# Block products for the input projections of a transformer layer, with q, k, v and pooled features kept in DRAM

## The chip, the core and the metric

The kernel runs on one core of a Trainium2 chip. The metric is the device time of one execution in microseconds (us), the median of several runs. The engines are TensorE (PE, with its weight loads as PEld), VectorE (DVE), ScalarE (ACT), GpSimd (POOL) and SyncE (SP, which issues most loads). Each engine works through its own list of instructions in a fixed order.

## What is computed

One layer over 1024 tokens of width 1024. A combined input projection feeds three token mixers; each has its output projection and a gate; the sum goes through w_out; a SwiGLU FFN follows.

```python
n = rmsnorm(h, norm_mix_pre)
proj = n @ w_in                     # 512 pool, 3 x 512 q k v, 256 xq, 3 x 1024 gates
gates = sigmoid(proj[..., o2:]).reshape(b, s, 3, d)
y_pool = pool_mixer(p_in, w_pool_mix, pool_scale) @ w_pool_o    # windows 2, 4, 8, 16
y_sb = stick_breaking_attention(q, k, v) @ w_sb_o               # 8 heads of 64, causal
y_x = memory_cross_attention(xq, rmsnorm(mem, norm_mem), w_mem_kv) @ w_x_o   # 4 heads, 256 tokens
merged = gates[:, :, 0] * y_pool + gates[:, :, 1] * y_sb + gates[:, :, 2] * y_x
h = h + rmsnorm(merged @ w_out, norm_mix_post)
gu = rmsnorm(h, norm_ffn_pre) @ w_ffn_in
h = h + rmsnorm((silu(gu[..., :D_FF]) * gu[..., D_FF:]) @ w_ffn_out, norm_ffn_post)
```

In the stick-breaking attention a weight is sigmoid(z_ts) times the product of (1 - sigmoid(z_tj)) over the keys between s and t; there is no softmax.

## The kernel before

Tokens are reversed in time and stand in two chunks c of 512 columns; features lie on partitions, in eight tiles k of 128. Precision comes from splitting: each operand is a high part (rounded to the matmul's format, ScalarE) and a low part (the rest, VectorE or POOL), and `mm3` issues three matmuls, lines 164 to 166:

```python
nc.tensor.matmul(ps, lh, rh, start=first, stop=False, skip_group_check=onto)
nc.tensor.matmul(ps, lh, rl, start=False, stop=False, skip_group_check=onto)
nc.tensor.matmul(ps, ll, rh, start=False, stop=last, skip_group_check=onto)
```

`split` (lines 145 to 160) loads a weight tile of 128 x 512 and makes its two halves, `wh` on ScalarE (L158) and `wl` (L159) on VectorE or, where the call says so, on POOL. `project` (from line 301) makes one tile of 128 output features for both chunks: 2 chunks x 8 k x 3 = 48 matmuls of 512 columns.

The stages, in the order of the program:

1. x is loaded, scaled and split while the pooling part of w_in is multiplied with it; the sum of squares gives the row scale (`rms_rows`, with `diag` at L190).
2. x is loaded again and normalised (`normalise`, L241 and L245) into the tiles nh and nl, beside the memory's K and V (mk, mv: matmuls of 256 columns).
3. xq (2 tiles by `project`), then the pool mixing (L399 to L428: window sums on VectorE, one small product, result in SBUF), then the memory attention: `scores` with a softmax made of two sigmoids and a reciprocal (L455 to L459), `recalled`.
4. The first branch's gates (8 tiles by `project`), each with its product with w_pool_o (12 matmuls a chunk).
5. V: 2 chunks x 8 k x 4 row blocks x 3 = 192 matmuls of 512 columns, result in SBUF.
6. The head loop, four head pairs p. Each projects q and k (`project`, `stack_q`, `stack_k`), then goes through eight units (t2, e). `sticks` makes the scores (L558, L559), two sigmoids, the scan on VectorE (L573) and the multiplication (L583); `values` transposes (L596), splits (L169, L170) and multiplies with V (L608, L611); L350 adds the halves. `sticks` runs one unit ahead of `values`. Gate tiles of the branches 1 and 2 stand between: one after the projections and the rest after the units. Finished gates go to DRAM.
7. The merge (from L642): the head outputs (oh, ol) with w_sb_o, the memory attention's (xo, from DRAM) with w_x_o, times the gates loaded from DRAM; then w_out.
8. The FFN, already in blocks of seven products (`product`, `opening`, and the loop after it).

What stands in which order on an engine is set by the tile scheduler, which follows the program's order, takes blocks under `tc.high_priority()` earlier, and keeps the loads that go through `load` in program order on SP's queue. Buffers come from pools (act 32, a 16, b1 8, b2 8, c 12, d 6, r 4 tiles; eight PSUM banks as pa 3, pz 2, pt 2, pv 1).

## Time and profile before

| | |
|---|---|
| runs | 1520.4 us median of 3 (1519.17 to 1521.04) |
| profiled execution, its own time | 1520.77 us |
| its span, first to last instruction | 1519.1 us |
| PE busy | 1470.4 us, 97% |
| VectorE busy | 1013.5 us, 67% |
| ScalarE busy | 693.8 us, 46% |
| POOL busy | 476.2 us, 31% |
| mean granted TensorE clock | 0.990 |
| moved by DMA | 203.23 MB, 134 GB/s |

Shares are of the span, the time between the first and the last instruction. The engines work side by side, so the shares don't add up; PEld is shown apart from PE since the weight load of one matmul can run beside the matmul ahead of it. A wait in the profile names the instruction that waits and, behind the arrow, the one that released it.

### The profile page before, as it was taken

The numbers are of one execution on the slowest core, as the hardware profiler recorded it, in microseconds if no ns is written. First come the engines' busy times: TensorE is split into PE (matmuls) and PEld (weight loads), VectorE is DVE, ScalarE is ACT, GpSimd is POOL, SyncE is SP. The second block draws the span as 40 slices with busy tenths as digits, with TensorE's granted clock in tenths as the row PEclk, the third lists the DMA queues.
The fourth block names the chain that finished last, engine by engine and source line by source line (L and its number), as shares of the span: only waits on it lengthen the run. The fifth ranks groups of instructions, "written<-read, shape, count | busy, mean of one in ns | idle before, by whom it ended". The sixth has DMA issues, their size and how long they took to land.

```text
span 1519.1 us, 20437 instructions
## 1 busy us (share of the span) xinstructions
PE 1470.4 (97%) x6878; PEld 1217.4 (80%) x6878; DVE 1013.5 (67%) x1552; ACT 693.8 (46%) x1375; POOL 476.2 (31%) x747
## 2 busy tenths in 40 slices
PE   9799999999999999998999989999999999999996
PEld 7678888888888888886788778888888887788875
DVE  8996996327687475766624478675566666578475
ACT  7454665235565454552234664223333333444452
POOL 7554342044454444445565530000011112000011
PEclk9999999999999999999999999999999999999998
DMA  6432222332231322217665453443465555664344
GB/s 223 133 99 67 70 90 79 107 100 71 56 84 49 90 60 69 68 55 230 199 201 178 156 189 118 157 142 125 132 194 194 193 187 201 231 192 146 105 152 160
DMA packets 101034, 203.23 MB, mean 134 GB/s; under 512 B 12720, under 2 KB 14272, under 8 KB 100928
## 3 DMA queue, kind: packets, MB, share of 16 engines
q1 hardware_dynamic: 81216, 147.36, 32.0%
q0 software_dynamic: 19136, 53.51, 10.2%
q8 instruction: 54, 0.88, 0.2%
q10 hardware_dynamic: 576, 1.05, 0.2%
...
HBM read 148.39 MB, written 48.76 MB: 130 GB/s over the span
## 4 chain that ended last, share of the span: by engine, by line
PE 82%; DVE 8%; DMA 4%; issue 3%; ACT 2%; POOL 1%; SPq 0%; DVEq 0%; POOLq 0%; ACTq 0%
PE pa L164 16%; PE pa L165 16%; PE pa L166 16%; PE pz L166 5%; PE pz L164 5%; PE pz L165 5%; PE pt L166 3%; PE pt L164 3%; PE pt L165 3%; PE pt L596 2%; PE pv L611 1%; PE pz L559 1%; PE pz L558 1%; PE pv L608 1%; DMA d<-gt 1%
## 5 line engine op out<-in xcount | busy, mean ns | idle before, releaser
L166 PE MATMUL pa<-act,wl 128*128 128x512 f32 (+1 forms) x716 | 280.7, 392 | 1.7 <-DVE wl L159 1.7
L165 PE MATMUL pa<-act,wh 128*128 128x512 f32 (+1 forms) x716 | 281.3, 393 | 0.0
L164 PE MATMUL pa<-act,wh 128*128 128x512 f32 (+1 forms) x716 | 280.4, 393 | 0.6 <-ACT act L708 0.6
L159 POOL TENSOR_TENSOR wl<-ws,wh 128x512 fp32r<-128x512 f32 x132 | 181.1, 1374 | 238.1 <-ACT wh L158 224.8
L158 ACT CAST wh<-ws 128x512 fp32r<-128x512 f32 (+1 forms) x199 | 122.9, 618 | 194.3 <-PE pa L165 59.5
L166 PEld LDWEIGHTS pa<-act,wl 128*128 128x128 f32 x716 | 135.4, 189 | 27.9 <-DVE wl L159 2.3
L164 PEld LDWEIGHTS pa<-act,wh 128*128 128x128 f32 x716 | 135.4, 189 | 26.9 <-ACT act L708 0.9
L165 PEld LDWEIGHTS pa<-act,wh 128*128 128x128 f32 x716 | 135.5, 189 | 25.4
L849 POOL DMA_DIRECT2D ff<-c x44 | 23.8, 540 | 222.9 <-DVE c L904 130.1
L159 DVE TENSOR_TENSOR wl<-ws,wh 128x512 fp32r<-128x512 f32 (+1 forms) x67 | 52.7, 789 | 59.5 <-ACT wh L158 38.6
L708 ACT CAST wh<-b 128x512 fp32r<-128x512 f32 x82 | 50.9, 620 | 88.2 <-PE pa L165 51.6
L169 ACT CAST d<-pt 128x512 fp32r<-128x512 f32 (+1 forms) x96 | 53.1, 559 | 70.9 <-PE pt L596 47.1
L170 DVE TENSOR_TENSOR d<-pt,d 128x512 fp32r<-128x512 f32 (+1 forms) x96 | 60.7, 637 | 34.6 <-ACT d L169 34.1
L708 ACT CAST d<-b 128x512 fp32r<-128x512 f32 x66 | 40.8, 621 | 93.8 <-PE pt L165 46.2
L709 DVE TENSOR_TENSOR d<-b,d 128x512 fp32r<-128x512 f32 x66 | 45.4, 691 | 54.5 <-ACT d L708 54.5
L573 DVE TENSOR_TENSOR_SCAN r<-d,zero 128x513 f32<-128x513 f32 (+1 forms) x64 | 60.1, 945 | 28.1 <-POOL d L566 27.6
L175 POOL TENSOR_TENSOR rc<-rv,mhalf 128x1 f32<-128x1 f32 (+2 forms) x15 | 14.5, 967 | 202.1 <-DVE rv L1011 199.4
L164 PE MATMUL pa<-a,wh 128*128 128x512 f32 x192 | 75.6, 395 | 0.8 <-DVE c L892 0.8
L166 PE MATMUL pa<-a,wl 128*128 128x512 f32 x192 | 75.0, 392 | 0.5 <-DVE wl L159 0.5
L708 ACT CAST wh<-ws 128x512 fp32r<-128x512 f32 x44 | 27.4, 622 | 90.3 <-DVE ws L883 45.7
L583 DVE TENSOR_TENSOR b<-b,r 128x512 f32<-128x512 f32 (+1 forms) x96 | 63.4, 669 | 7.4 <-ACT d L169 0.5
L709 DVE TENSOR_TENSOR wl<-b,wh 128x512 fp32r<-128x512 f32 x82 | 56.2, 685 | 15.1 <-ACT wh L708 10.5
...
## 6 DMA issues: line engine op xcount, KB each, us to landing
b<-in_w_ffn_in_dram SPq DMA_DIRECT2D x88, 256.0 KB, 2.7
ws<-in_w_gate_dram SPq DMA_DIRECT2D x48, 256.0 KB, 2.6
gt<-g POOLq DMA_DIRECT2D x48, 256.0 KB, 2.8
d<-gt SPq DMA_DIRECT2D x48, 256.0 KB, 3.4
ws<-in_w_ffn_in_dram SPq DMA_DIRECT2D x44, 256.0 KB, 2.7
ff<-c POOLq DMA_DIRECT2D x44, 256.0 KB, 3.1
b<-ffS SPq DMA_DIRECT2D x44, 256.0 KB, 2.6
b<-ff SPq DMA_DIRECT2D x33, 256.0 KB, 3.2
```

The lines of the kernel that those rows point to most:

```text
L158: nc.scalar.copy(wh[:, :n], ws[:, :n])
L159: lo.tensor_sub(wl[:, :n], ws[:, :n], wh[:, :n].bitcast(F32))
L164: nc.tensor.matmul(ps, lh, rh, start=first, stop=False, skip_group_check=onto)
L165: nc.tensor.matmul(ps, lh, rl, start=False, stop=False, skip_group_check=onto)
L166: nc.tensor.matmul(ps, ll, rh, start=False, stop=last, skip_group_check=onto)
L169: nc.scalar.copy(hi, ps)
L170: nc.vector.tensor_sub(lo, ps, hi.bitcast(F32))
L573: nc.vector.tensor_tensor_scan(ex[:, lo : C + 1], rest[:, lo : C + 1], zero.broadcast_to([P, C + 1 - lo]), 1.0 if c == i // 4 else carry[i ...
L583: nc.vector.tensor_mul(sg[:, lo:], sg[:, lo:], carry[i][:, lo:C])
L596: nc.tensor.transpose(ptr[:, col + n * P : col + (n + 1) * P], att[i, j // 4][:, (j % 4) * P : (j % 4 + 1) * P], ident,)
L708: nc.scalar.copy(hi, src)
L709: eng.tensor_sub(lo, src, hi.bitcast(F32))
```

## The change

The blocks. The normalised x is no longer one set of tiles but a 2 x 2 matrix of blocks (first index: chunk; second: half of the features), and four sums of blocks are made beside it: S1 = 21 + 22, S2 = S1 - 11, S4 = 12 - S2, S3 = 22 - S2. Two neighbouring weight tiles over both chunks are then made of seven products (`pairs`), each with 4 k x 3 = 12 matmuls of 512 columns; sums of weight blocks are made on VectorE, halves of the weights on VectorE or POOL. xq, q, k and the first branch's gates go this way, 1 + 2 + 2 + 4 pairs. V does too (`v_product`), with V's weights as the moving operand in halves of 256 columns.

DRAM. Raw pooled features, xq, q, k, v and the mixed pool features (with their low parts) are written to DRAM by POOL's queue and come back through SP's: `fetch(p, c)` brings a head pair's q and k in loads of 64 rows, `pooled` and `recall` their own.

Order. Three gate half tiles (`early`) run before the sums are made. Memory attention and pool mixing become steps (`aside`) that run between products. The gates of branches 1 and 2 become 58 steps of 12 matmuls, 4 ahead of the heads, 46 inside them in proportion to the transposes of a unit, 8 behind. The product with w_pool_o stands in the merge. Softmax takes one Exp per block with its sum, then a multiplication by the reciprocal of that sum. In `sticks` the ones and the carry are set by POOL in the scan's result and no longer in its input.

```diff
@@ the blocks of x; normalise() goes
+    A = {n: [None] * HK for n in ("11", "12", "21", "22", "S1", "S2", "S3", "S4")}
+    def normed_x(k, c, t):
+        load(t, x[k, c])
+        nc.vector.scalar_tensor_tensor(t, t, gain(G_PRE, k), rbc[c], ALU.mult, ALU.mult)
+        return t
...
+    early(0)
+    sums, a22 = [None] * HK, [None] * HK
+    for q in range(HK):
+        room = t_d if q < 3 else t_r
+        sums[q], a22[q] = normed_x(q, 1, room()[:, :C]), normed_x(q + HK, 1, room()[:, :C])
+        nc.vector.tensor_add(sums[q], sums[q], a22[q])
+        A["S1"][q] = parts(sums[q], t_act(), t_act(), nc.vector if q % 2 else nc.gpsimd)
+    xq_raws = [quarters(w_xq, 0)]
+    early(1)
+    xq_raws.append(quarters(w_q, 0))
+    early(2)
+    for q in range(HK):
+        nc.vector.tensor_sub(sums[q], sums[q], a11[q])
+        A["S2"][q] = parts(sums[q], t_a(F32R), t_a(F32R))
...
@@ two weight tiles by seven products
+    def opening(raw, sink):
+        (b11, b12), (b21, b22) = raw
+        X, Y = ps_a(), ps_a()
+        product(X, w_parts(b11, nc.gpsimd), "11", True)
+        p1 = copied(X)
+        product(Y, w_parts(b21, nc.gpsimd), "12", True)
+        nc.vector.tensor_add(p1, Y, p1)
+        sink(0, 0, p1)
+        return X
+
+    def pairs(jobs, raws=None, pool=("S4", "S3", "22")):
...
+            X, Y = opened[j], ps_a()
+            t = b11
+            nc.vector.tensor_sub(t, b12, t)
+            product(Y, some(t, "S1"), "S1", True)
+            s5 = copied(Y)
+            aside()
+            nc.vector.tensor_sub(t, b22, t)
+            product(X, some(t, "S2"), "S2")
+            s2 = copied(X)
+            product(Y, some(b22, "S4"), "S4")
+            nc.vector.tensor_add(s2, Y, s2)
+            sink(0, 1, s2)
+            aside()
+            nc.vector.tensor_sub(b12, b22, b12)
+            product(X, some(b12, "S3"), "S3")
+            nc.vector.tensor_add(s5, X, s5)
+            sink(1, 1, s5)
+            nc.vector.tensor_sub(b21, b21, t)
+            if len(opened) == j + 1 < len(jobs):
+                opened.append(opening(raws[j + 1], jobs[j + 1][1]))
+            product(X, some(b21, "22"), "22")
+            sink(1, 0, X)
+            aside()
...
@@ q, k, xq to DRAM and back
+    def to_parts(dst, m):
+        def sink(c, i, t):
+            hi, lo = parts(t, t_d(F32R)[:, :C], t_d(F32R)[:, :C])
+            for u, d in zip((hi, lo), dst[m + i][c]):
+                nc.gpsimd.dma_start(d, u)
+        return sink
+    def stacked(dst, src, e):
+        r = slice(e * HD, (e + 1) * HD)
+        load(dst[:HD], src[e][r])
+        load(dst[HD:], src[1 - e][r])
...
@@ softmax
-            nc.scalar.activation(ew[:, :MEM], z[:, :MEM], AF.Sigmoid, bias=st[:, 0:1], scale=SCALE)
-            nc.vector.reciprocal(ew[:, MEM:], ew[:, MEM:])
...
+            nc.scalar.activation(
+                ew[:, zs], z[:, zs], AF.Exp, bias=st[:, 2 + i : 3 + i], scale=SCALE,
+                accum_out=st[:, 4 + i : 5 + i],
+            )
...
@@ V
+                mm3(
+                    ps, ah[:, bs], al[:, bs], wh[:, qs], wl[:, qs],
+                    first and k == 0 and b % 2 == 0, k == HK - 1, not first or b % 2 == 1,
+                )
...
@@ heads
-        accs = project(w_q, p, lo=nc.gpsimd)
...
-        gates(todo[first[p] : first[p] + 1])
...
+    def stick_unit(p, t2, e):
+        if (t2, e) == (0, 0):
+            fetch(p, 1)
+        if (t2, e) == (2, 0) and p < 3:
+            fetch(p + 1, 0)
+        return sticks(*heads[p], t2, e)
...
+        done += share[t2]
+        upto = inside * done // total
+        fill(upto - filled)
+        filled = upto
...
@@ merge
+            pp_ = ps_t()
+            for q in range(4):
+                qs = slice(q * P, (q + 1) * P)
+                mm3(pp_, pwh[:, qs], pwl[:, qs], ph[q][c], pl[q][c], q == 0, q == 3)
...
+            nc.vector.tensor_mul(gt[0], pp_, gt[0])
```

Three places where the order of an engine's list is another. First VectorE ahead of the memory's V, before; `wl_847` is the low half of the first weights of V of the memory, L241 and L245 are the normalisation and its low parts, L409 the window sums of the pool mixing:

```order
L241 SCALAR_TENSOR_TENSOR d_830<-d_830,g_sb_99,r_458 128x512
L159 TENSOR_TENSOR wl_787<-ws_784,wh_786 128x512
L241 SCALAR_TENSOR_TENSOR d_837<-d_837,g_sb_99,r_458 128x512
L245 TENSOR_TENSOR act_820<-d_816,act_819 128x512
L409 TENSOR_TENSOR c_1106<-c_648 128x527
L409 TENSOR_TENSOR c_1126<-c_647 128x527
L409 TENSOR_TENSOR c_1143<-c_650 128x527
L159 TENSOR_TENSOR wl_847<-ws_844,wh_846 128x512
L241 SCALAR_TENSOR_TENSOR d_880<-d_880,g_sb_99,r_521 128x512
L245 TENSOR_TENSOR act_834<-d_830,act_833 128x512
```

and in the changed kernel, where L256 and L251 are the normalisation and its low parts, L195 the scale's diagonal and L164 the low halves of weights:

```order
L256 SCALAR_TENSOR_TENSOR d_633<-d_633,g_sb_99,r_458 128x512
L256 SCALAR_TENSOR_TENSOR d_640<-d_640,g_sb_99,r_458 128x512
L251 TENSOR_TENSOR act_504<-c_500,act_503 128x512
L191 TENSOR_SCALAR rv_732<-pt_457 128x2
L164 TENSOR_TENSOR wl_785<-ws_782,wh_784 128x512
L251 TENSOR_TENSOR act_518<-c_514,act_517 128x512
L251 TENSOR_TENSOR act_630<-d_626,act_629 128x512
L251 TENSOR_TENSOR act_644<-d_640,act_643 128x512
L195 TENSOR_SCALAR r_736<-ident_101,rc_734 128x128 x2
L164 TENSOR_TENSOR wl_803<-ws_800,wh_802 128x512
L164 TENSOR_TENSOR wl_835<-ws_832,wh_834 128x512
L164 TENSOR_TENSOR wl_853<-ws_850,wh_852 128x512
```

The window sums and the second chunk's normalisations no longer stand between the low halves.

Second PE in the last head pair, before; L596 are transposes, L608 and L611 the products with V, L164 to L166 the merge's products, which the scheduler drew in between:

```order
L608 MATMUL pv_7061<-d_7067,a_3225 128x256
L611 MATMUL pv_7061<-d_7066,a_3225 128x256
L608 MATMUL pv_7061<-d_7067,a_3219 128x128
L611 MATMUL pv_7061<-d_7066,a_3219 128x128
L608 MATMUL pv_7061<-d_7080,a_3237 128x256
L611 MATMUL pv_7061<-d_7079,a_3237 128x256
L608 MATMUL pv_7061<-d_7080,a_3231 128x256
L611 MATMUL pv_7061<-d_7079,a_3231 128x256
L165 MATMUL pa_7524<-b2_7441,wh_7480 128x512
L166 MATMUL pa_7524<-c_7440,wl_7481 128x512
```

and in the changed kernel, where L887 are transposes and L899 and L902 the products with V:

```order
L887 MATMUL pt_7383<-ident_101,b2_7243 128x128
L887 MATMUL pt_7383<-ident_101,b2_7254 128x128
L887 MATMUL pt_7383<-ident_101,b2_7243 128x128
L899 MATMUL pv_7289<-d_7295,a_5788 128x256
L902 MATMUL pv_7289<-d_7294,a_5788 128x256
L899 MATMUL pv_7289<-d_7295,a_5790 128x128
L902 MATMUL pv_7289<-d_7294,a_5790 128x128
L899 MATMUL pv_7289<-d_7308,a_5784 128x256
L902 MATMUL pv_7289<-d_7307,a_5784 128x256
L899 MATMUL pv_7289<-d_7308,a_5786 128x256
L902 MATMUL pv_7289<-d_7307,a_5786 128x256
```

Here transposes and products with V follow one another without any other work between.

Third PE at the passage to the merge, before; `pz` is the memory attention's product with w_x_o, `b1` its operand from DRAM:

```order
L166 MATMUL pz_7503<-b1_7456,wl_7475 128x512
L164 MATMUL pz_7503<-b1_7460,wh_7474 128x512
L608 MATMUL pv_7120<-d_7126,a_3237 128x256
L611 MATMUL pv_7120<-d_7125,a_3237 128x256
L608 MATMUL pv_7120<-d_7126,a_3231 128x128
L611 MATMUL pv_7120<-d_7125,a_3231 128x128
L165 MATMUL pz_7503<-b1_7461,wh_7474 128x512
L166 MATMUL pz_7503<-b1_7460,wl_7475 128x512
```

and in the changed kernel, where `pt` is the product with w_pool_o, `a` its operand from DRAM, and `pa` the head outputs' product with w_sb_o:

```order
L899 MATMUL pv_7472<-d_7478,a_5784 128x256
L902 MATMUL pv_7472<-d_7477,a_5784 128x256
L899 MATMUL pv_7472<-d_7478,a_5786 128x128
L902 MATMUL pv_7472<-d_7477,a_5786 128x128
L169 MATMUL pt_7728<-a_7618,wh_7648 128x512
L170 MATMUL pt_7728<-a_7620,wh_7648 128x512
L169 MATMUL pt_7776<-a_7652,wh_7648 128x512
L170 MATMUL pt_7776<-a_7654,wh_7648 128x512
L171 MATMUL pa_7741<-c_7668,wl_7643 128x512
L169 MATMUL pa_7741<-c_7672,wh_7642 128x512
```

The memory attention's product comes later, and the pool product stands among the first of the merge.

## Rows read from the trace of the kernel before

**Rows 1.** Page, part 1: busy time, share of the span and instructions of each engine.

```profile
PE 1470.4 (97%) x6878; PEld 1217.4 (80%) x6878; DVE 1013.5 (67%) x1552; ACT 693.8 (46%) x1375; POOL 476.2 (31%) x747
```

**Rows 2.** By stage: length; busy (count) PE, PEld, DVE, ACT, POOL; clock, DMA share, GB/s.

```profile
48.00:120.00 72.00, 62.55 (x296) 52.46 (x296) 71.50 (x104) 34.21 (x64) 40.88 (x32) 0.93 0.40 114
...
120.00:340.00 220.00, 219.99 (x1060) 183.91 (x1059) 139.80 (x261) 104.42 (x223) 66.49 (x130) 1.00 0.29 86
...
340.00:680.00 340.00, 339.41 (x1811) 290.07 (x1810) 230.46 (x316) 182.99 (x396) 153.03 (x312) 1.00 0.24 65
...
680.00:760.00 80.00, 71.83 (x314) 57.13 (x313) 51.49 (x78) 21.30 (x40) 42.07 (x39) 0.98 0.68 214
...
925.00:1280.00 355.00, 355.00 (x1568) 293.98 (x1567) 232.42 (x366) 122.48 (x211) 43.17 (x80) 1.00 0.52 169
```

**Rows 3.** PE's timeline: first and last of a run of 256-column matmuls.

```profile
68.09 0.28 PE L164 MATMUL pa<-act,wh 128*128 128x256 f32 x1
...
70.12 0.28 PE L166 MATMUL pa<-act,wl 128*128 128x256 f32 x1
```

**Rows 4.** Groups by form: weight loads, busy time, mean ns, idle before.

```profile
L165 PEld LDWEIGHTS pa<-act,wh 128*128 128x128 f32 x716 | 135.5, 189 | 25.4
```

**Rows 5.** PE's waits: line, releaser; us in total, times, longest.

```profile
PE pa L165 <- DVE wl L159: 5.1, 2, 4.1
...
PE pt L194 <- DVE r L190: 4.1, 2, 2.4
...
PE pa L164 <- DVE d L683: 3.4, 2, 2.9
...
PE pz L165 <- DMA b<-xo: 2.9, 2, 2.0
...
PE pa L164 <- ACT c L647: 1.3, 1, 1.3
```

**Rows 6.** VectorE's timeline, from the normalisations' start to the awaited weight half.

```profile
46.97 2.73 DVE L241 SCALAR_TENSOR_TENSOR d<-d,g_sb,r 128x512 f32<-128x512 f32 x4
...
73.84 0.68 DVE L159 TENSOR_TENSOR wl<-ws,wh 128x512 fp32r<-128x512 f32 x1
```

**Rows 7.** Groups of the page and by form: busy, mean ns, idle before.

```profile
L459 DVE RECIPROCAL c<-c 128x256 f32<-128x256 f32 x32 | 54.4, 1727 | 2.6 <-ACT c L455 2.2
...
L709 DVE TENSOR_TENSOR wl<-b,wh 128x512 fp32r<-128x512 f32 x82 | 56.2, 685 | 15.1 <-ACT wh L708 10.5 <-issue 4.0
...
L159 POOL TENSOR_TENSOR wl<-ws,wh 128x512 fp32r<-128x512 f32 x132 | 181.1, 1374 | 238.1 <-ACT wh L158 224.8
...
L573 DVE TENSOR_TENSOR_SCAN r<-d,zero 128x513 f32<-128x513 f32 (+1 forms) x64 | 60.1, 945 | 28.1 <-POOL d L566 27.6
...
L583 DVE TENSOR_TENSOR b<-b,r 128x512 f32<-128x512 f32 (+1 forms) x96 | 63.4, 669 | 7.4 <-ACT d L169 0.5
...
L170 DVE TENSOR_TENSOR d<-pt,d 128x512 fp32r<-128x512 f32 (+1 forms) x96 | 60.7, 637 | 34.6 <-ACT d L169 34.1
...
L573 DVE TENSOR_TENSOR_SCAN r<-d,r,zero 128x513 f32<-128x513 f32 x32 | 41.5, 1302 | 7.8 <-ACT d L562 7.8
...
L350 DVE TENSOR_TENSOR b<-pv,t 64x256 f32<-64x256 f32 x32 | 13.4, 420 | 31.5 <-ACT t L349 31.1
...
L849 POOL DMA_DIRECT2D ff<-c x44 | 23.8, 540 | 222.9 <-DVE c L904 130.1 <-DVE c L890 92.7
```

**Rows 8.** Chain that ended last: eight transposes of the head loop in a row.

```profile
374.76 0.87 PE pt L596 x8
```

**Rows 9.** Engines in a stretch of the memory attention, columns as in rows 2.

```profile
160.00:200.00 40.00, 40.00 (x211) 34.03 (x210) 38.93 (x71) 25.42 (x58) 14.07 (x32) 1.00 0.20 64
```

**Rows 10.** Timelines of VectorE and of POOL at 626 us, head loop.

```profile
626.50 1.40 DVE L583 TENSOR_TENSOR b<-b,r 128x384 f32<-128x384 f32 x1
...
625.78 1.69 POOL L159 TENSOR_TENSOR wl<-ws,wh 128x512 fp32r<-128x512 f32 x1 [0.20 <-ACT wh L158]
```

**Rows 11.** DMA issues of the page: x, KB each, median us to landing.

```profile
d<-gt SPq DMA_DIRECT2D x48, 256.0 KB, 3.4
```

More of the change, by code (lines that the diff above doesn't have):

```diff
@@ new lines, in hybrid_block, with fetch @@
+    to_values(0, 1, s2)
+    aside()
+    sub2(b12, b22, b12)
+    v_product(X, two(b12), "S3")
+    for i in range(2):
+        nc.vector.tensor_add(s5[i], X[i], s5[i])
+    to_values(1, 1, s5)
+    aside()
+    sub2(b21, b21, b11)
+    v_product(X, two(b21), "22")
+    to_values(1, 0, X)
+    while background:
+        aside()
+    heads = {}
+    def fetch(p, c):
+        if c == 0:
+            heads[p] = [[[None] * NC for _ in range(2)] for _ in range(3)]
+        qst, kh, kl = heads[p]
+        for e in range(2):
+            for tiles in (qst, kh, kl):
+                tiles[e][c] = t_c(F32R)[:, :C]
+            stacked(qst[e][c], q_d[p][c], e)
+            twice(kl[e][c], k_d[p][c][1], e)
+            twice(kh[e][c], k_d[p][c][0], e)
+        if p % 2 == 0 and c == 1:
+            for j in range(KT - 1, -1, -1):
+                v = v_sb[j][p // 2] = t_a(F32R)
+                load(v, v_d[j][p // 2])
@@ new lines, in hybrid_block @@
+    mix_h, mix_l = split(w_mix)
+    background += [pooled(g, c) for g in range(4) for c in (1, 0)] + [lambda: fetch(0, 0)]
+    pairs([(lambda m=m: quarters(w_gate, m), to_gate(0, m)) for m in range(0, KT, 2)], pool=())
+    for q in range(HK):
+        u = normed_x(q, 1, t_d()[:, :C])
+        A["21"][q] = parts(u, t_act(), t_act())
+    later = [
+        (b * KT + m, half, c)
+        for b in (1, 2)
+        for m in range(KT)
+        for half in range(2)
+        for c in range(1 if b == 1 and m < EARLY else 0, NC)
+    ]
@@ new lines, in hybrid_block, with gate_load, fill @@
+    gate_units = list(dict.fromkeys((t, half) for t, half, _ in later))
+    gate_w = {}
+    def gate_load():
+        if gate_units:
+            t, half = gate_units.pop(0)
+            ws = wpool.tile([P, C], F32, tag="ws", name="ws", bufs=3)
+            load(ws, w_gate[t, half])
+            gate_w[t, half] = ws
+    def fill(n):
+        for _ in range(n):
+            t, half, c = later.pop(0)
+            if gate_w[t, half].__class__ is not tuple:
+                gate_w[t, half] = w_parts(gate_w[t, half], nc.gpsimd)
+                gate_load()
+            gate_step(t, half, c, gate_w[t, half])
@@ new lines, in hybrid_block @@
+    fill(FILL_FIRST)
+    inside = len(later) - FILL_LAST
+    done = filled = 0
+    share = [15, 11, 7, 3]
+    total = 2 * 4 * sum(share)
+    o_sb = [[None] * NC for _ in range(4)]
+    units = [(p, t2, e) for p in range(4) for t2 in range(4) for e in range(2)]
+    def stick_unit(p, t2, e):
[4 more added lines that the diff above has]
+        return sticks(*heads[p], t2, e)
+    ahead = stick_unit(*units[0])
@@ L641, in hybrid_block @@
+    merge_w = []
+    fill(len(later))
+    for c in range(NC):
+        for g in range(4):
+            for dst, d in zip((ph, pl), ph_d[g][c]):
+                dst[g][c] = t_a(F32R)
+                load(dst[g][c], d)
+        if c == 0:
+            w_merge(0)
     oh = [[None] * NC for _ in range(4)]
```

483 lines of the change are left out of this document (281 added, 202 removed).

## The prediction

> **What bounds the kernel now.** The profile was read from the coarse to the fine: the page's busy times, the time by stage, PE's list of waits, then timelines of single stretches. TensorE is busy for 97% of the span, VectorE for 67% [rows 1]. The table by stage says where the missing 3% lies [rows 2]. From 120 to 340 us (projections, memory attention, first gates) PE has no gap, and none from 925 to 1280 (FFN); in the head loop (340 to 680) it lacks 0.6 of 340 us. The gaps before the FFN are at 48 to 120 us (9.45 us idle, clock 0.93) and at 680 to 760 (8.2 us idle, clock 0.98). So a matmul saved in a gapless stretch shortens the run by its spacing, and work saved on another engine by nothing. In the FFN 1568 matmuls of 512 columns take 355.0 us: 0.2264 us each [rows 2]. Those of 256 columns, at the full clock, follow one another in 0.1194 us (17 intervals from 68.09 to 70.12) [rows 3], half of it.
>
> **The matmuls.** In blocks, two weight tiles over both chunks take 7 products of 12 matmuls, not 96. Pairs: xq 1, q 2, k 2, first gates 4; 9 x 12 = 108 matmuls of 512 columns fewer. V loses its 192 and gets 7 products x 4 row blocks x 4 k x 3 = 336 of 256 columns. The product with w_pool_o (16 x 12) moves from the gates to the merge, its count as before. Sum: -300 x 0.2264 = -67.9, +336 x 0.1194 = +40.1, so **-27.8 us**. V alone gives 3.4 of them, since its 1/8 fewer columns come in twice as many matmuls, each with a weight load. That spacing hides the load: one is recorded at 189 ns, over 119 [rows 4].
>
> The Trainium skill (TensorE: Matmul & The Clock Gate, "The mechanism" in Part 3) says that a weight load overlaps matmuls in flight only when the row groups differ. By that, each of V's would cost 0.189 + 0.119, 336 of them 103.5 us, and the sum would be 63 us higher, slower than before; [rows 3, 4] speak against it, since those loads fill all rows and are hidden.
>
> **Start (48 to 120 us).** PE's longest waits are here: 5.1 us for a low weight half from VectorE, 4.1 us for the scale's diagonal [rows 5]. Between 46.97 and 73.84, the awaited half, VectorE runs normalisations and the pool mixing's multiplications and sums [rows 6]. The order shows the pool mixing gone from here and only eight normalisations left, about 10 us of work in place of 27. At stake are 9.45 us idle and about 5 us of half clock (7% of 72): 14.5. What comes late next are the sums S1 to S4, which all four pieces of VectorE, ScalarE and POOL work must make before the pairs; three gate tiles (72 matmuls, 16 us) lie ahead of them as cover. I take **-10**, nearer to the whole than to nothing, as the row that waited longest goes; bounds 0 and -14.5.
>
> **Softmax and pool mixing.** Of VectorE's work 32 reciprocals at 1.73 us go, 54 us [rows 7]; two more activation-table loads come. Both lie where PE has no gap: 0. The pairs add VectorE and POOL work: per pair (84 matmuls, 19.0 us of PE) 13 VectorE operations at 0.69 = 9.0 us, on POOL 5 subtractions at 1.37 and 8 stores at 0.54 = 11.2 [rows 7]. Covered, with the background steps between; without cover, VectorE would add some 9 us a pair. Stores and reloads through DRAM bring some 40 MB (80 tiles of 256 KB out, as much back in) to a stretch that moved 41 (220 us at 86 GB/s, 340 at 65), a DMA share of about 0.5; the FFN has no gap at 0.52 [rows 2]: 0.
>
> **Head loop.** Here the cover shrinks. PE's own part: 288 transposes at 0.109 [rows 8], 256 matmuls of 256 columns, 96 of 512, the rest by width, 103 us. Gate pieces: 58 x 12 x 0.2264 = 158. In all 261 us, where before the q and k projections and more gates made it 340. VectorE's part stays: scans 60.1 + 41.5, multiplications 63.4, lows 60.7 less 16 x 0.68 for memory attention, additions 13.4: 228 us [rows 7], 87% of 261 where it was 68% of 340. Walking through PE's order with these durations, VectorE's due work runs ahead of PE's in three stretches without gate pieces: the middle of the second head pair (37.3 us of PE to 46.6 of VectorE), the end of the third (25.1 to 35.9) and of the fourth (5.6 to 18.4): 9, 11 and 13 us. Scores are made one unit ahead, which absorbs part; before, such rises were 3 to 5 us and cost 0.6 in 340. I take **+15**, about half; bounds 0 and +33. A fetch lands in about 3.4 us [rows 11], and one unit of attention or a gate piece (2.7 us) lies ahead of each: four bare ones would cost 14, within the bounds.
>
> **Merge (680 to 760 us).** PE waits 2.9 us for the memory attention's tiles from DRAM, 3.4 for a VectorE product or half, 1.3 for ScalarE [rows 5]. Sixteen pool products (16 x 12 x 0.2264 = 43 us, moved, not added) now come with it: the order puts the first of them among the last values, and a block of the merge asks for 2.15 MB in 13.6 us instead of 1.9 MB in 8.2. At stake are 8.2 us idle and 1.6 of clock. I take **-5**, since the one of 2.9 us for VectorE, ahead of w_out, is not touched; bounds 0 and -8. New joints between stages (pairs to V, V to pairs, first fetch): **+3**, from waits of 0.6 to 1.3 us for single operands [rows 5]; bounds 0 and +8.
>
> **Sum.** -27.8 - 10 + 15 - 5 + 3 = -24.8. The profiled execution took 1520.8 us (span 1519.1), 0.4 over the median of 1520.4, so the same sum serves both: **1496 us**, 1.6% faster. About 0.2% (3 us) is what a measurement of this kernel tells from no change.
>
> **Rivals.**
> 1. *The gaps come back elsewhere* (0.2). The S sums are late by as much as the weights were, the merge waits for 2.15 MB a block: only the matmuls and half of start and merge are won. -27.8 - 4 + 18 + 3 = -11, **1510**. For it: the start's VectorE is busy for 71.5 of 72 us [rows 2], and S1 is the first thing that the pairs use. Against it: 16 us of gate matmuls ahead.
> 2. *The head loop keeps PE full* (0.2). -27.8 - 12 + 0 - 5 + 3 = -42, **1479**. For it: at 160 to 200 us VectorE was busy for 38.93 of 40 us and PE for all 40 [rows 9]. Against it: there PE's work did not depend on that of VectorE unit by unit.
> 3. *VectorE becomes the bound of the head loop* (0.06), the slower side. A multiplication of 384 columns took 1.40 us where a POOL subtraction lay beside it (POOL's ran from 625.78 to 627.47) [rows 10]; the mean of all 96 is 0.67 [rows 7]. If every one took 1.40, that is 96 x 0.73 = 70 more: VectorE 298 us, at a share of 0.97 a stretch of 307, so +46: -27.8 - 10 + 46 - 5 + 3 = +6, **1527**. It goes over to slower where the loop loses 40, that is from 292 us of VectorE, 0.67 us more for each multiplication. Against it: POOL has two wide subtractions for a gate tile, as before, and the mean says that few multiplications met one.
> 4. *The removed matmuls are not on the path* (0.04): projections wait for VectorE or POOL for as long as they got shorter, **1519**. Against it: 9.0 and 11.2 of 19 us.
>
> The Trainium skill (SBUF — State Buffer, "Who interferes with whom") says that a VectorE instruction with two SBUF inputs and a GpSimd instruction that reads SBUF exclude one another for the whole instruction. That is rival 3's mechanism, and the 1.40 us agree; which of the two waits it leaves to the order of issue. By its rule, with every one of the 96 hit and losing, the time would be 1527; the mean of 0.67 us bears out a small part of that.
>
> **How the numbers follow.** My forecast has 0.5, rival 1 and 2 each 0.2, rival 3 0.06, rival 4 0.04. The bounds: start and merge at their best and no loss in the heads give 1470, the heads' +33 alone 1514, with half of start lost 1519. The range of 8 in 10 reaches to both neighbours, **1474 to 1515**. Faster by over 0.2%: the forecast, rivals 1 and 2, less a little for a stack of losses in one of them, 0.89; within: 0.04; slower: 0.07.
>
> **What would show it.** Matmuls of 512 columns down by 300, of 256 up by 336, V's at 0.12 us. Between 48 and 120 us under 5 us idle, none of it for a weight half. In the pairs PE without gaps. In the head loop VectorE at 80 to 85%, and PE waiting 10 to 20 us in all for the multiplication before a transpose or for the lows before a value, most of it where no gate pieces lie. In the merge no wait for the memory attention's tiles. Wrong, if V's matmuls come at over 0.2 us, if PE waits in the pairs for S sums over 10 us, or if multiplications in the head loop have a mean over 1.2 us.

## The result and the profile after

| | before | changed |
|---|---|---|
| median | 1519.8 us | 1535.2 us |
| profiled execution (span) | 1520.8 (1519.1) | 1532.7 (1531.0) |
| granted clock, mean | 0.990 | 0.984 |

The ratio is 1.0097, with a 95% interval of 1.0074 to 1.012: 1% slower, where 1.6% faster had been forecast. One run of the changed kernel was disturbed (5106 us) and is left out; the other three lie between 1532.7 and 1536.9 us.

To see where the time went, the trace of both kernels was cut at the first 256-column matmul, the last one of the memory's V, the first score and the last value product. In each part every matmul was counted at its undisturbed spacing (0.227 us for 512 columns, 0.175 for 384, 0.1195 for 256, 0.109 for 128): that is the work. What its start and the next one's start lie further apart is the loss (waits, half clock, late starts). The 1.1 us ahead of the first matmul and the 14.8 us from the start of the last one on are the same in both kernels and stand in no part.

| part | before: work + loss | changed: work + loss | change of the loss |
|---|---|---|---|
| up to the memory's K | 49.3 + 9.6 | 49.3 + 10.2 | +0.6 |
| K and V of the memory | 12.0 + 12.4 | 11.6 + 0.3 | -12.1 |
| from there to the first score | 256.2 + 4.3 | 247.3 + 43.9 | +39.6 |
| heads | 341.9 + 5.2 | 271.1 + 28.4 | +23.2 |
| merge to the end | 779.1 + 33.2 | 831.3 + 21.7 | -11.5 |
| sum | 1438.5 + 64.7 | 1410.6 + 104.5 | +39.8 |

The work fell by 27.9 us, the loss rose by 39.8: +11.9, which is the difference of the spans. Matmuls of 512 columns fell from 5776 to 5476 and those of 256 rose from 514 to 850, as forecast. The rest of this text is about the 39.8.

The busy times of the page of the changed kernel, against [rows 1]:

```profile
PE 1453.5 (95%) x6914; PEld 1201.0 (78%) x6914; DVE 1042.6 (68%) x1593; ACT 705.2 (46%) x1405; POOL 530.2 (35%) x754
```

The same view by stage as [rows 2] (length; busy and count of PE, PEld, DVE, ACT, POOL; clock, DMA share, GB/s), first over the old stretch from 48 to 120 us, then over the parts as they lie now:

```profile
48.00:120.00 72.00, 53.13 (x256) 43.30 (x255) 68.76 (x74) 33.03 (x63) 47.82 (x42) 0.86 0.43 139
...
73.00:123.00 50.00, 31.16 (x109) 23.52 (x108) 49.97 (x50) 19.77 (x37) 32.09 (x22) 0.76 0.29 98
...
123.00:364.00 241.00, 228.45 (x1237) 195.69 (x1236) 175.40 (x328) 125.73 (x268) 112.15 (x141) 0.99 0.54 164
...
364.00:663.00 299.00, 282.12 (x1536) 236.55 (x1535) 224.48 (x321) 173.93 (x384) 144.50 (x291) 0.99 0.40 128
...
663.00:770.00 107.00, 107.00 (x463) 87.30 (x463) 55.46 (x77) 22.05 (x37) 50.65 (x43) 0.99 0.63 198
```

Between 73 and 123 us PE issues only 109 matmuls, at a clock of 0.76, and VectorE is never free: 49.97 of 50 us for 50 operations, a mean of 1.0 us where [rows 7] show 0.69 for a subtraction of that size. The merge (663 to 770) has no gap any more; before, it had two of the longest waits of [rows 5].

PE's waits (line, releaser; us in total, times, longest), against [rows 5]:

```profile
PE pa L169 <- ACT g L512: 10.3, 1, 10.3
...
PE pa L169 <- ACT wh L250: 6.1, 5, 2.3
...
PE pa L169 <- DVE d L532: 5.0, 1, 5.0
...
PE pv L899 <- DVE b L371: 4.6, 5, 1.6
...
PE pt L887 <- DVE d L175: 3.3, 4, 1.5
...
PE pv L899 <- DVE d L175: 3.1, 5, 1.4
...
PE pa L169 <- DVE d L357: 2.4, 1, 2.4
...
PE pz L589 <- DMA r<-xq: 2.2, 1, 2.2
```

The 5.1 us for the low weight half and most of the 4.1 for the diagonal are gone, as is the wait for `xo`. In their place stand 10.3 us for a gate's sigmoid (L512), 5.0 put down to a block of a sum (L532), and in the heads the addition that frees the bank of the values (L371) and the low parts (L175).

The name L532 misleads. The matmul that waits, at 83.26 us, belongs to the second gate tile, which needs no sum; what it needs is the high half of its weights, and the cast of that (L163) ended at the same moment. ScalarE's timeline:

```profile
82.06 0.62 ACT L250 CAST act<-d 128x512 fp32r<-128x512 f32 x1 [4.64 <-DVE d L525]
...
82.59 0.61 ACT L163 CAST wh<-ws 128x512 fp32r<-128x512 f32 x1
```

The cast stands behind one that waited for VectorE's sum S1 (L525) until 82.06, and its own weights had landed only at 81.05, behind the eight x tiles and four xq weights on SP's queue.

V's matmuls in the new form, PE's timeline, first and last of 33 in a row:

```profile
234.23 0.28 PE L169 MATMUL pa<-wh,act 128*128 128x256 f32 x1
...
238.07 0.28 PE L171 MATMUL pa<-wh,act 128*128 128x256 f32 x1
```

32 intervals in 3.84 us: 0.120 us each, as in [rows 3].

What happened at 85 us, first VectorE's timeline, where L536 is the subtraction for S4 and L251 a low part:

```profile
83.76 1.76 DVE L251 TENSOR_TENSOR act<-r,act 128x512 fp32r<-128x512 f32 x1
...
85.44 1.75 DVE L536 TENSOR_TENSOR c<-act,d 128x512 f32<-128x512 f32 x1
...
87.12 5.60 DVE L536 TENSOR_TENSOR c<-act,d 128x512 f32<-128x512 f32 x1
...
92.64 0.68 DVE L532 TENSOR_TENSOR d<-d,c 128x512 f32<-128x512 f32 x1
```

and POOL's over the same stretch (L164 and L251 are low parts, L513 a store):

```profile
84.93 1.72 POOL L164 TENSOR_TENSOR wl<-ws,wh 128x512 fp32r<-128x512 f32 x1
...
86.59 0.56 POOL L513 DMA_DIRECT2D gt<-g  x1
...
87.18 1.29 POOL L164 TENSOR_TENSOR wl<-ws,wh 128x512 fp32r<-128x512 f32 x1
...
88.41 3.76 POOL L251 TENSOR_TENSOR act<-d,act 128x512 fp32r<-128x512 f32 x3
```

POOL is never free from 84.93 to 92.2 us, and from 87.18 on it does four subtractions in a row. A subtraction of VectorE that takes 0.69 us alone took 5.60 from 87.12 on: it ended 0.55 us after the last of POOL's. From 94.6 to 107 us the two engines took turns instead, seven operations each, every one 1.7 to 1.8 us long; one of either:

```profile
97.93 1.75 POOL L164 TENSOR_TENSOR wl<-ws,wh 128x512 fp32r<-128x512 f32 x1
...
98.44 1.78 DVE L251 TENSOR_TENSOR a<-d,a 128x512 fp32r<-128x512 f32 x1
```

Over the part from 58 to 123 us VectorE's operations took 65.4 us; at the shortest tenth of the times that operations of the same form take in this trace they would take 40.1.

### The profile page after: what moved, and what is told of

It is laid out like the page before. It is cut to its first block, busy times and chain, and to the rows that moved or that the text cites. A ratio compares the mean times of both kernels' runs of the same rounds, so it can differ in the third digit from the quotient of the medians.

```text
span 1531.0 us, 21083 instructions
## 1 busy us (share of the span) xinstructions
PE 1453.5 (95%) x6914; PEld 1201.0 (78%) x6914; DVE 1042.6 (68%) x1593; ACT 705.2 (46%) x1405; POOL 530.2 (35%) x754
## 4 chain that ended last, share of the span: by engine, by line
PE 74%; DVE 10%; issue 5%; DMA 4%; POOL 3%; ACT 3%; SPq 1%; POOLq 0%; DVEq 0%; ACTq 0%
PE pa L169 14%; PE pa L171 14%; PE pa L170 14%; PE pz L171 5%; PE pz L169 5%; PE pz L170 5%; PE pt L169 3%; PE pt L171 3%; PE pt L170 3%; DVE r L868 2%; DMA ws<-in_w_gate_dram 1%; PE pt L887 1%; POOL wl L251 1%; PE pv L169 1%; PE pv L170 1%
## 5 line engine op out<-in xcount | busy, mean ns | idle before, releaser
L169 PE MATMUL pa<-act,wh 128*128 128x512 f32 (+1 forms) x572 | 227.1, 397 | 24.7 <-ACT g L512 10.3
L170 PE MATMUL pa<-act,wh 128*128 128x512 f32 (+1 forms) x572 | 225.2, 394 | 0.0
L171 PE MATMUL pa<-act,wl 128*128 128x512 f32 (+1 forms) x572 | 223.0, 394 | 2.2 <-POOL wl L164 2.2
L250 ACT CAST wh<-b 128x512 fp32r<-128x512 f32 x159 | 98.2, 621 | 164.2 <-PE pa L170 104.1
L169 PEld LDWEIGHTS pa<-act,wh 128*128 128x128 f32 x572 | 109.2, 191 | 49.2 <-ACT g L512 10.7
L163 ACT CAST wh<-ws 128x512 fp32r<-128x512 f32 (+1 forms) x121 | 74.0, 612 | 119.9 <-PE pa L170 33.6
L164 POOL TENSOR_TENSOR wl<-ws,wh 128x512 fp32r<-128x512 f32 x74 | 98.2, 1331 | 88.1 <-ACT wh L163 86.4
L170 PEld LDWEIGHTS pa<-act,wh 128*128 128x128 f32 x572 | 109.3, 191 | 21.0
L251 DVE TENSOR_TENSOR wl<-b,wh 128x512 fp32r<-128x512 f32 x116 | 84.3, 727 | 19.0 <-ACT wh L250 14.6
L251 DVE TENSOR_TENSOR d<-b,d 128x512 fp32r<-128x512 f32 x66 | 45.3, 689 | 53.1 <-ACT d L250 52.9
L170 PE MATMUL pa<-b,wh 128*128 128x512 f32 x196 | 77.4, 395 | 1.5 <-DVE b L225 1.5
L868 DVE TENSOR_TENSOR_SCAN r<-a,zero 128x512 f32<-128x512 f32 (+1 forms) x64 | 57.2, 898 | 25.7 <-POOL a L856 25.5
L251 POOL TENSOR_TENSOR wl<-b,wh 128x512 fp32r<-128x512 f32 x43 | 58.8, 1372 | 44.6 <-ACT wh L250 36.6
L175 DVE TENSOR_TENSOR d<-pt,d 128x512 fp32r<-128x512 f32 (+1 forms) x96 | 60.1, 635 | 12.0 <-ACT d L174 11.3
L874 DVE TENSOR_TENSOR b<-b,r 128x512 f32<-128x512 f32 (+2 forms) x96 | 61.3, 643 | 6.7 <-POOL b L856 0.5
```

The costliest lines, as they stand in the source:

```text
L163: nc.scalar.copy(wh[:, :n], ws[:, :n])
L164: lo.tensor_sub(wl[:, :n], ws[:, :n], wh[:, :n].bitcast(F32))
L175: nc.vector.tensor_sub(lo, ps, hi.bitcast(F32))
L250: nc.scalar.copy(hi, src)
L251: eng.tensor_sub(lo, src, hi.bitcast(F32))
L868: nc.vector.tensor_tensor_scan(ex[:, lo + 1 : C + 1], rest[:, lo:], zero.broadcast_to([P, C - lo]), start, ALU.mult, ALU.add,)
```

## The experiments

Times are medians. Ratios are to the kernel before, run on the same chip in the same batch. Between runs of different batches the difference of the medians and that of the ratios lie up to 2 us apart.

**e1: another bank for the early gates.** PE's longest wait looks like one for a bank. ScalarE's timeline shows how the sigmoid came late: it stands behind a cast that waits for VectorE's sum of weights (L461).

```profile
116.50 0.62 ACT L250 CAST wh<-b 128x512 fp32r<-128x512 f32 x1 [3.02 <-DVE b L461]
...
117.03 0.59 ACT L512 ACTIVATE g<-pa 128x512 f32<-128x512 f32 x1
```

```diff
-            gate_accs[t, c] = ps_a()
+            gate_accs[t, c] = ps_z() if t < KT + EARLY and c == 0 else ps_a()
```

> The three early gate tiles accumulate in the pz banks instead of pa. Theory A: the 10.3 us wait at 107 to 118 us is only for a pa bank that ScalarE frees late (its list holds the gate's sigmoid behind a cast that waits for VectorE), while the products that wait need no sum: the wait falls under 3 us and the run is 7 to 10 us shorter than the changed kernel (about 1525). Theory B: VectorE is late with all sums, and PE meets it a product or two later: the wait shows up in front of the S1 or S2 product, under 4 us are won (about 1531).

1535.6 us, ratio 1.0104 (1.008 to 1.0128): nothing won. The first two rows of PE's waits of this run:

```profile
PE pa L169 <- ACT wh L250: 12.6, 6, 8.5
...
PE pz L169 <- ACT wh L163: 5.1, 1, 5.1
```

PE gets one product further and there waits 8.5 us in one piece for the cast of a weight, which stands behind VectorE's sum of weights. The second row is the 5.0 us of the changed kernel, here under the name of the gate weight's cast. Theory A falls, theory B holds: VectorE is late, and the bank was only where PE met it.

**e2: low parts from POOL to VectorE.**

```diff
-        A["S1"][q] = parts(sums[q], t_act(), t_act(), nc.vector if q % 2 else nc.gpsimd)
+        A["S1"][q] = parts(sums[q], t_act(), t_act())
...
-        A["S4"][q] = parts(u, t_a(F32R), t_a(F32R), nc.gpsimd)
+        A["S4"][q] = parts(u, t_a(F32R), t_a(F32R))
...
-        A["22"][q] = parts(a22[q], t_act(), t_act(), nc.gpsimd)
+        A["22"][q] = parts(a22[q], t_act(), t_act())
```

(and `split` of the early gates' weights without `lo=nc.gpsimd`)

> The low parts of S1, S4, block 22 and of the early gates' weights (16 subtractions) go from POOL to VectorE. Theory C: VectorE's 65 us between 58 and 123 us are only 40 of its own; POOL's subtractions stretch the rest, 0.68 us to 1.7: with them gone, 40 + 16 x 0.68 = 51 us, the sums are ready some 10 us earlier and the run is 7 to 14 us shorter (1520 to 1527). Theory D: VectorE simply has too much to do before the pairs: 16 x 0.68 = 11 us are added to it, the run is up to 11 us longer (to 1544).

1523.3 us, ratio 1.0025 (1.001 to 1.004): 12 us shorter than the changed kernel (11 by the ratios), by giving the engine that was full 16 more operations. The loss up to the first score fell from 43.9 to 32.2 us; of it that before the pairs run freely (73 to 123 us there, 73 to 113 here) from 25.9 to 14.2, the rest stayed at 18.0. What went is the wait of 10.3 us with the slow matmuls behind it: from 106 to 123 us the changed kernel lost 13.1, from 98 to 113 this run loses 1.5. The wait for the second gate tile's weights stayed, 4.3 us. By stage:

```profile
73.00:113.00 40.00, 31.04 (x116) 23.98 (x115) 37.66 (x60) 18.60 (x36) 13.86 (x9) 0.87 0.41 137
```

60 operations now take 37.7 us, 0.63 each. VectorE's timeline from 88 us, first and last of eleven in a row, and what follows:

```profile
88.55 0.69 DVE L251 TENSOR_TENSOR act<-d,act 128x512 fp32r<-128x512 f32 x1
...
94.57 0.69 DVE L540 TENSOR_TENSOR d<-d 128x512 f32<-128x512 f32 x1
...
96.41 1.76 DVE L461 TENSOR_TENSOR b<-b,b 128x512 f32<-128x512 f32 x1 [1.15 <-POOL wl L251]
```

and what POOL does meanwhile:

```profile
89.49 6.89 POOL L251 TENSOR_TENSOR wl<-b,wh 128x512 fp32r<-128x512 f32 x1 [9.49 <-ACT wh L250]
```

Now VectorE goes without a break until 95.3 us, and a subtraction of POOL that takes 1.3 us alone took 6.89, until 96.4. The exclusion works both ways: in these two stretches the engine with the unbroken list goes on and the other one stands.

**e3: six early gate tiles.** `EARLY = 6`, with three more calls of `early`.

> Six early gate half tiles instead of three: 72 more matmuls (16 us) ahead of the sums, as many fewer among the heads. If the start lacks only cover, the 10.3 and 5.0 us waits fall to under 4 in all and the head loop, with 6 gate pieces fewer, loses 3 to 8 us more: 5 to 12 us shorter than the changed kernel. If ScalarE and VectorE are held up by the gates' own casts and low parts, the start is as long as before and the time the same or longer.

1543.2 us, ratio 1.0141 (1.0106 to 1.0175): 8 us longer. The loss up to the first score is 43.9 us as before, with 16.4 us more work in it; the heads have 16.4 less and lose 35.0 instead of 28.4. More gates ahead of the sums cover nothing; that the gates' own casts and low parts hold up the sums is the likely reason, which no run shows by itself.

**e4: two banks for the values.**

```diff
-        po = ps_v()
+        po = ps_v() if e == 0 else ps_a()
```

> The sums of the values alternate between the pv bank and a pa bank in the head loop. PE waits there 4.6 us for the addition that frees the one pv bank. If this wait stands by itself, 3 to 5 us are won; if VectorE is the bound of the head loop, the wait moves to the low parts or to the multiplication and nothing is won (within 1.5 us).

1554.3 us, ratio 1.0229 (1.0209 to 1.025): a miss of both, 19 us longer. The wait for the bank is gone, but the scheduler now moved gate pieces behind the heads (their work fell from 271 to 248 us), and PE waits for low parts:

```profile
PE pa L899 <- DVE d L175: 12.5, 7, 3.2
...
PE pv L899 <- DVE d L175: 11.1, 10, 3.3
```

As a test of the bank it is no use. It speaks for the cover (23 us less work among the heads, 23.5 us more loss, 28.4 to 51.9), but the second bank stands beside that, so it does not show it alone.

**e5: the remaining low parts of the first pairs to VectorE too.**

```diff
-        product(X, w_parts(b11, nc.gpsimd), "11", True)
+        product(X, w_parts(b11), "11", True)
...
-        product(Y, w_parts(b21, nc.gpsimd), "12", True)
+        product(Y, w_parts(b21), "12", True)
...
-        xq_raws,
+        xq_raws, (),
```

> On top of e2, the low parts of the weights in the openings and in the xq and q pairs go to VectorE as well, so that POOL has no wide subtraction left between 73 and 125 us. In e2 three POOL subtractions took 9.8 us behind VectorE's unbroken list, and PE waited 4.0 us for one of them. If the exclusion works both ways, that wait goes and the run is 3 to 6 us shorter than e2 (about 1518 to 1520). If VectorE, now with some 18 subtractions more, is the bound of the start, the wait only changes its name: within 2 us of e2 or longer.

1521.5 us, ratio 1.0004 (0.999 to 1.0018), less than e2 by 1.8 (by 3 going by the ratios): between the two expectations. The wait for POOL's low part is gone, but the loss from 73 us to the pairs is still 13.0 (14.2 in e2). Of it 7.3 us lie between 78 and 93 us, at the wait of 4.3 for the second gate tile's weights. ScalarE's timeline shows that this is a late load:

```profile
82.87 0.62 ACT L163 CAST wh<-ws 128x512 fp32r<-128x512 f32 x1 [3.00 <-DMA ws<-in_w_gate_dram]
```

The other 5.7 lie between 103 and 114 us, at waits of 2.1 us for an addition of VectorE that empties a bank and of 1.5 for a weight's cast; VectorE's 70 operations fill 40.7 of the 41 us.

**e6: no early gates.** On e2, `EARLY = 0` and no call of `early`.

> On top of e2, no gate tile runs ahead of the sums; 72 matmuls (16 us) go to the pieces among the heads. Three more early tiles had left the loss at the start at 44 us and cost 6.6 us in the heads. If the early gates cover nothing at the start since their own loads, casts and low parts delay the sums, the start loses no more than in e2 (32 us) and the heads 4 to 8 us less: 1515 to 1519. If they do cover, the start loses up to 12 us more: 1527 to 1532.

1532.0 us, ratio 1.0073 (1.0052 to 1.0094): 9 us longer than e2 (7 by the ratios). Three tiles do cover: without them the start loses 24.3 us (14.2 in e2). The heads, with 26.5 us more work, lose 24.4 (29.0). So three were worth having, and the three more of e3 were not.

**e7: without the multiplication in the heads.**

```diff
-                nc.vector.tensor_mul(sg[:, lo:], sg[:, lo:], carry[i][:, lo:C])
```

> The multiplication of the sigmoid by the scan's result is left out of the heads (96 operations, 61 us of VectorE); the scans stay. The heads lost 28 us of PE in the changed kernel, 5 before. If VectorE's share (87% of PE's work there) is the cause, the loss falls under 12 us and the run is 15 to 22 us shorter than the changed kernel (1513 to 1520). If the loss is of latencies (one bank for the values, transposes that wait for a split, late gate weights), less than 8 us are won.

1525.2 us, ratio 1.0031 (1.0021 to 1.0041): 10 us won, between the two. VectorE's operations in the heads, 239.8 us in sum, became 178.3, the loss 17.8. Some 10 of the 28 us hang on this multiplication, by its amount of work or as a link between the scan and the transposes, which the run does not tell apart; the larger rest remains when VectorE has a quarter less to do.

**e8: the gates' low parts among the heads to VectorE.** On e2:

```diff
-                gate_w[t, half] = w_parts(gate_w[t, half], nc.gpsimd)
+                gate_w[t, half] = w_parts(gate_w[t, half])
```

> On top of e2, the low parts of the gate weights among the heads (29) go from POOL to VectorE, 29 x 0.68 = 20 us more for it. In the heads VectorE's operations are stretched by 22 us in all. If the gates' subtractions on POOL make most of that, VectorE is no worse off and the time stays within 3 us of e2 (1523); if POOL's triangle selections make it, VectorE gets 10 us or more on top where it already has 87% of PE's time, and the run is 5 to 12 us longer.

1521.6 us, ratio 1.0007 (0.9992 to 1.0022). VectorE got 32 subtractions of 0.69 us, 22 us, and its operations in the heads took 5 us longer in sum (241.2 to 246.4): POOL's subtractions had cost VectorE some 17 us here too. PE lost 26.4 instead of 29.0.

**e9: the second early gate ahead of the sums.** On e5, `early(1)` right behind `early(0)`.

> On top of e5, the second early gate tile stands ahead of the second chunk's normalisation, so that its weights are asked for before the eight x tiles on SP's queue. In e5 PE waited 4.3 us at 79 us for that tile's high half, whose load landed late. If this wait stands by itself, 3 to 5 us are won against e5 (about 1517); if the x tiles and with them the sums come later by as much, nothing is won (within 1.5 us of 1521.5).

1528.1 us, ratio 1.0058 (1.0037 to 1.008): 7 us longer than e5, against both. The wait moved on to the third gate tile (5.2 us, up to 90.2), and the heads, which the edit does not touch, lose 34.5 us (28.9 in e5); the scheduler dealt out their work anew, and no run shows more of the cause.

**e10: ScalarE empties the values' bank.** On e5:

```diff
-        nc.vector.tensor_add(dst[own], ps[own, :n], t[own, :n])
+        nc.scalar.copy(dst[own], ps[own, :n])
+        nc.vector.tensor_add(dst[own], dst[own], t[own, :n])
```

> On top of e5, ScalarE copies both halves of the values' sum out of the bank, and VectorE adds them in SBUF; the one pv bank is then free without VectorE. PE waits 5.1 us in the heads and 1.9 in the memory attention for that addition. If these are latencies of the bank, the run is 4 to 7 us shorter than e5 (1515 to 1517); if VectorE is the bound there, the waits move to the lows of the transposes and under 2 us are won.

1530.5 us, ratio 1.0056 (1.003 to 1.0082), between 1523.7 and 1532.1: no gain, and the heads lose 35.5 us (28.9 in e5). The wait for the addition went, and that for the low parts, 1.0 us in e5, took its place:

```profile
PE pv L900 <- DVE d L175: 8.4, 11, 2.2
```

**e12: e9, e10 and e8 together.**

> e9 and e10 together, and the low parts of the gates among the heads on VectorE (e8). If each takes a wait of its own, 1510 to 1515, faster than the kernel before (1520); if they share one cause, VectorE's list, it stays within 3 us of the best of them.

1514.2 us, ratio 0.9965 (0.995 to 0.998): faster than the kernel before. The heads lose 21.7 us.

**e13: e12 without e9's move.**

> e12 without the gate loads that were moved ahead (e9 had lost 6 us by itself, mostly in the heads): e2's and e5's low parts, e8's gate lows and e10's addition. If POOL's wide subtractions are what stretched VectorE in the heads too, the heads lose no more than in e12 (22 us) and the start a little less: 1510 to 1514, faster than the kernel before. If e12's gain came from the moved loads, about 1521 to 1528.

1514.2 us, ratio 0.9963 (0.9951 to 0.9975): the same, so the gain is not that of the moved loads. The change from e10 to this run is e8's one line: 8 us by the spans of the profiled executions (1521.9 and 1513.7; that of e10 is the fastest of its five), 16 by the medians, 14 by the ratios. With the same work in the heads, 276.2 us, they lose 21.3 instead of 35.5. Scans and multiplications of 512 columns in the changed kernel, from 364 to 650 us (busy, mean ns, idle before):

```profile
L868 DVE TENSOR_TENSOR_SCAN r<-a,r,zero 128x512 f32<-128x512 f32 x32 | 44.9, 1406 | 17.5 <-ACT a L852 17.4
...
L874 DVE TENSOR_TENSOR b<-b,r 128x512 f32<-128x512 f32 x48 | 40.2, 839 | 3.2 <-ACT b L853 0.2
```

the same of e10, in its heads (349 to 660 us):

```profile
L869 DVE TENSOR_TENSOR_SCAN r<-a,r,zero 128x512 f32<-128x512 f32 x32 | 43.1, 1356 | 8.0 <-ACT a L853 7.9
...
L875 DVE TENSOR_TENSOR b<-b,r 128x512 f32<-128x512 f32 x48 | 41.4, 862 | 2.8
```

and the same of this run (364 to 650 us), with the gates' low parts that VectorE now has:

```profile
L869 DVE TENSOR_TENSOR_SCAN r<-a,r,zero 128x512 f32<-128x512 f32 x32 | 40.8, 1278 | 5.4 <-ACT a L853 5.2
...
L875 DVE TENSOR_TENSOR b<-b,r 128x512 f32<-128x512 f32 x48 | 33.3, 695 | 2.8
...
L251 DVE TENSOR_TENSOR wl<-ws,wh 128x512 fp32r<-128x512 f32 x32 | 21.7, 687 | 10.3 <-ACT wh L250 10.2
```

From e10 a scan fell from 1356 to 1278 ns and a multiplication from 862 to 695, some 10 us for these 80 operations (from the changed kernel 11), against 21.7 us of new subtractions; VectorE's busy time in the heads rose by 3.5 us only (226.2 to 229.7). So POOL's low parts do stretch VectorE's work here; how much of the 14 us of loss hangs on that and how much on the order that the scheduler deals is not told apart.

**e14: the mixing's product one step later.** On e13, each step of the background makes the operand of one small product and issues the product of the step before.

> On top of e13, each small product of the pool mixing stands one step later than the VectorE work that makes its operand. PE waits 4.3 us for the operand of one such product and 1 to 3 us for others between 320 and 350 us. If PE's fixed order, with a product that stands too early, is the cause, 3 to 6 us go (1507 to 1510); if VectorE is late with all it does there, the wait moves to the next weight sum and under 1.5 us go.

1516.1 us, ratio 0.998 (0.997 to 0.999): nothing won, the wait is 5.1 us. The wait is not for the product's operand, as both expectations took it (this one and that of e15), but for the one pv bank: it holds the product before until VectorE has taken that one's low part (L688 of e13, L695 here), and a step more between operand and product does not bring that forward. VectorE's timeline of e13 at that place (L669 is a window sum):

```profile
315.87 0.69 DVE L669 TENSOR_TENSOR c<-c 128x521 f32<-128x521 f32 x1
...
322.98 2.21 DVE L669 TENSOR_TENSOR c<-c 128x521 f32<-128x521 f32 x1
...
329.27 3.68 DVE L251 TENSOR_TENSOR wl<-b,wh 128x512 fp32r<-128x512 f32 x2
...
332.87 0.74 DVE L688 SCALAR_TENSOR_TENSOR d<-pv,g_sb,d 128x512 fp32r<-128x512 f32 x1
```

and POOL's, with window sums of the fourth group:

```profile
326.05 4.21 POOL L669 TENSOR_TENSOR c<-c 128x527 f32<-128x527 f32 x3 [1.43 <-PE pa L170]
```

A window sum of 0.69 us took 2.21 a little later, and two low parts of 0.69 took 3.68, where POOL has its part of the mixing (the fourth group) in hand. L688 stands behind them and ended at 333.6; the awaited product started at 333.75.

**e15: all of the pool mixing on VectorE.** On e13:

```diff
-            adder = nc.vector if g < 3 else nc.gpsimd
+            adder = nc.vector
```

> On top of e13, the fourth group's window sums and multiplications (10 operations of 512 columns and a little more) go from POOL to VectorE. e14 won nothing, so the product does not stand too early in PE's list; its operand is late. In e13 VectorE's operations between 323 and 335 us took 1.55 to 2.21 us where those of POOL lay beside them. If that is the cause of the 4.3 us wait at 329 us, it falls under 1.5 us and the run is 2 to 5 us shorter than e13 (1509 to 1512); if VectorE has too much to do at that place, 10 x 0.68 = 7 us more make it longer.

1517.6 us, ratio 0.9982 (0.997 to 0.9994). The 4.3 us wait is gone, and the loss up to the first score fell from 31.7 to 25.2: it was POOL's part of the mixing that made VectorE late there. The time is 3 us longer all the same, because the heads, which the edit does not touch, lose 29.8 instead of 21.3. Their scans and multiplications of 512 columns are as short as in e13 (a multiplication 0.69 us), so POOL's subtractions of weights are not behind this loss.

## Why the prediction was wrong, step by step

By the parts of the table, with 3.2 of the 4.3 us in its third row lost up to 120 us, the terms came out like this: matmuls -27.9, start +11 (forecast -10), pairs and joints +17 (forecast +3), heads +23 (forecast +15), merge -11.5 (forecast -5). The start is the largest miss (21 us), the pairs and joints the second (14).

- **Matmuls, -27.8.** The work fell by 27.9, and V's matmuls come at 0.120 us. The rule of the Trainium skill (TensorE: Matmul & The Clock Gate, "The mechanism" in Part 3), by which the loads of V would have been added, does not hold for them: 33 matmuls, each with a load of its own, stand in a row at the spacing that hides it.
- **Start, -10.** Half of it was right: the part with the memory's K and V lost 12.4 us and loses 0.3. The step that failed is the sentence on what is late next: that the sums would be made behind three gate tiles as cover. It compared 16 us of PE's matmuls with nothing, though the sums' work could be counted in the code: 8 normalisations, 20 sums and differences and 20 low parts, 38 of these 48 on VectorE. From 73 to 123 us, with the end of the memory's V and the first sums of weights, it had 50 operations, most of 0.69 us if undisturbed, and POOL 19 subtractions of 1.3 beside them. PE loses 25.9 us there. About 12 of that is the exclusion of VectorE and POOL (e2: 60 operations of VectorE in 37.7 us, where 50 had filled 50). Some 7 to 8 lie at the second gate tile: the cover itself came late, since its weights' load is late (7.3 us in e5, with no POOL subtraction left on that stretch), and asking for them earlier moved the wait to the third tile (e9). Only the rest, 5.7 us in e5, is left for the amount of VectorE's work.
- **Pairs, softmax, joints, +3.** The loss from 123 us to the first score is 18.0, where the kernel before lost 1.1 behind 120 us: +17, outside the bound of +8, so this term failed too. It priced the joints by single operands and the background steps at nothing. PE's waits there add up to 12.6 us. The pairs' own banks and operands make 3.2 of them, nearly covered, as forecast; the rest are waits of 0.4 to 2.4 us at V's split (2.4), the xq tile from DRAM (2.2) and the steps of memory attention and mixing. In e13 6 us of such loss went when POOL's part of the mixing did (e15); the rest was not taken apart.
- **Head loop, +15.** It is +23.2, within the bounds of 0 and +33, with VectorE at 224.5 of 299 us, 75%, below the forecast 80 to 85. PE's work came to 271 us, near the 261 of the forecast. The reading of the order (too little cover) is borne out in part: the runs with less work among the heads mostly lose more (298 us of it lost 24, 271 lost 28, 255 lost 35, 248, with e4's banks, lost 52; before, 342 lost 5), but among runs with 275 to 276 us of it the loss goes from 21 (e13) over 29 (e5) and 35 (e9) to 36 (e10), so that work alone does not set it. Of the 28.4 us half lies in the three stretches that were named (middle of the second pair 5.3, end of the third 2.5, end of the fourth 6.7), the other half is spread over all pairs. That POOL's low parts stretch scans and multiplications was put down as a rival; e13 shows the stretching, not what it costs.
- **Merge, -5.** The loss from the merge on fell by 11.5, more than the bound of 8: the waits for `xo` and for ScalarE went, and that of 2.9 us for VectorE ahead of w_out as well, which the prediction had left standing.
- **Rivals.** Rival 1 (gaps come back elsewhere) is what happened at the start and in the pairs, but it was priced too low: it still gave start and merge a gain together (-4, though half of the forecast's 15 would be -7.5), when the start alone lost 11; and the merge, where it saw waits for DRAM, won 11.5. Rival 4's 1519 does not follow either: without the matmuls' -27.8 the forecast's other terms give 1524. It did not happen, since the work fell as counted. Rival 3 had the right mechanism in the wrong place: the exclusion was priced in the heads, where it is one part, and not where the change puts VectorE and POOL side by side on the same block. The rule of the Trainium skill (SBUF — State Buffer, "Who interferes with whom") that it cites agrees with e2 and with the rows at 85 us; a VectorE subtraction of 0.69 us took up to 5.6, one of POOL of 1.3 took 6.9.

What stays open: most of the loss between the start and the heads, some 12 us that no run took apart, why the merge won more than its bound, and how much of the heads' loss lies in the order that the scheduler deals. Runs whose edit touches nothing in the heads can differ there by 6 to 9 us (e5 and e9, e13 and e15), so an effect of that size on the whole time is not shown by one edit.

## What to carry to other kernels

When matmuls are saved by sums of operands, count the operations that make the sums on the engine that makes them, and lay that time against the matmuls that run meanwhile; an operand that all products share has no cover but what stands ahead of it, and that cover needs its own weights in time. Splitting elementwise work between VectorE and POOL was no gain where both read two operands from SBUF on the path: moving POOL's share to the full engine made the run 12 us shorter. The name of a wait can mislead: a matmul that waited for a gate weight's cast bore the name of a sum that ended at the same moment. Work that is taken out of a stretch where PE hides another engine has to be counted as lost cover, too.
